# The SSM groups' matrix products in plain float32, with a shorter table of steps, in a hybrid encoder layer

## The chip, the cores and the metric

The kernel runs on one core of one Trainium2 chip. The time is device microseconds from the start to the end of an execution; the table below gives the median of three runs, and the profiled execution has a time of its own.

## The reference, cut to what matters

One encoder layer on an input of 4096 tokens and 1024 channels, all float32. A combined projection feeds three branches (a state space model, a pooling branch, windowed attention); their gated outputs are joined and projected back. The change concerns the first branch alone: 16 groups of 16 channels, each with 64 complex states in two directions.

```python
h = rms_norm(x, pre_g)
su, sg, pu, pg, q, k, v, ag = jnp.split(h @ w_in, IN_SPLITS, axis=-1)
...
bu_re = jnp.einsum('blgp,gnp->blgn', u, bb_re)
bu_im = jnp.einsum('blgp,gnp->blgn', u, bb_im)
_, _, h_re, h_im = lax.associative_scan(
    _complex_linear_combine, (lam_re, lam_im, bu_re, bu_im), reverse=reverse, axis=1)
return (jnp.einsum('blgn,gpn->blgp', h_re, c_re)
        - jnp.einsum('blgn,gpn->blgp', h_im, c_im))
...
y = jnp.concatenate([y_ssm, y_pool, y_attn], axis=-1) @ w_out
return x + rms_norm(y, post_g)
```

## The kernel before, in words

The tokens are cut into 8 blocks of 512. Matrix products keep close to float32 accuracy by splitting each operand into a high part of type float32r and the rest, a low part, and adding three products: high by high, high by low, low by high. `split` (line 187) does that: a copy on ACT writes the high part, and `lo_part` (line 184) subtracts it on DVE or, where the call says so, on POOL. `mm3` (line 989, its products on lines 990 to 992) issues the three products.

The program runs in four phases: two of input projections (the second with the attention), the remaining gate projections (`p3_block`, line 1129), and the output products (`w_out_k`, line 1278, lines 1287 to 1289) with the final norm. An order written by hand interleaves them: `Slots` (from line 84) holds a queue of steps for each slot, and `e.step()` issues the steps of one slot. `chunk` (line 354) issues six projection products of 128x512 and then takes one step, so a slot is six products of PE and whatever was queued for it. Each engine executes its instructions in the order in which they were issued.

`to_p3` (line 1397) runs at slot 422 and queues the 16 groups by `ssm_group` (line 994), each starting `SSM_PACE`, 8, slots after the one before it. The table at the end of `ssm_group` says which step of a group is issued how many slots after its start. Eight consecutive tokens form a chunk, so that a group works on tiles of 128 partitions by `NC`, 512, columns: `load` brings a record `rec` (the group's matrices and angles) and the input `u` by two DMAs on SP's queue; `inputs_hi`, `wb_lo`, `ur_lo` split both; `turns` (POOL) and the `angle_` steps (ACT) make cosines and sines `cs`; `inputs_mm` makes the real and imaginary inputs `vr` and `vi` in PSUM, `direct_mm` starts the output `y`; `turn_re`, `turn_im`, `turn_sum` rotate them (four products on DVE, two sums on POOL); `scan` runs the recurrence along the columns, two instructions of 64 partitions each time (lines 1069 and 1071, DVE); `back_cos` (DVE), `back_sin` and `back_sum` (POOL) rotate back; `state_hi`, `state_lo` split the states `h`; `state_mm` adds their products to `y`; `out_copy` and `store` bring it out. In the trace `tt` shows as line 162 and `copy` as line 173.

The gate projections run from slot 384 to 575, the output products from slot 576. Near the end of that phase `y_pool` (line 1172, started at slot 546) and `y_attn` (line 1209) put the pooling branch's and the attention's operands together on POOL, DVE and ACT, and `load_wo` (line 1115) loads and splits the weights of the output product. Of other parts the text names `pr` (line 451) and `kp` (lines 659 and 661), two places where the program before already multiplies plain float32 operands, of 128 columns.

Of the kernel before, what the change touches and what calls it, by code (L numbers as in the profile page):

```python
# [11 lines left out]
F32R = mybir.dt.float32r  # L12
# [4 lines left out]
P = 128  # L17
# [8 lines left out]
NC = SEQ // L  # L26
# [9 lines left out]
REC = 689  # L36
# [93 lines left out]
def hybrid_kernel(ctx, tc, A, out):  # L130
    nc = tc.nc
    V, S, PL, T = nc.vector, nc.scalar, nc.gpsimd, nc.tensor
    dma = nc.sync.dma_start
# [4 lines left out]
    swd = tc.dram_tile([G, P, REC], F32, name="swd")  # L138
# [22 lines left out]
    def tt(eng, out, in0, in1, op):  # L161
        return eng.tensor_tensor(out=out, in0=in0, in1=in1, op=op)  # L162
# [9 lines left out]
    def copy(out, in_):  # L172
        return S.activation(out=out, in_=in_, func=AF.Copy)  # L173

    def bank(i, shape, nm):
        return banks[i].tile(shape, F32, tag="b", name=nm)

    def bc(ap, shape):
        return ap.to_broadcast(shape)

    def f(ap):
        return ap.bitcast(F32)

    def lo_part(lo, src, hi, eng):
        tt(eng, lo, src, f(hi), ALU.subtract)

    def split(hi, lo, src, eng, lag=1, scale=None):

        copy(hi, src)
        if lag:  # L190
            e.at(e.now + lag, lo_part, lo, src, hi, eng)
        else:
            lo_part(lo, src, hi, eng)
# [795 lines left out]
    def mm3(o, wh, wl, r, first, last):  # L989
        T.matmul(o, lhsT=wh, rhs=r[:, 0], start=first, stop=False)  # L990
        T.matmul(o, lhsT=wh, rhs=r[:, 1], start=False, stop=False)
        T.matmul(o, lhsT=wl, rhs=r[:, 0], start=False, stop=last)

    def ssm_group(g, R, t0):


        sv = R["sv"]
        rho = bc(R["rho"][:, g:g + 1], [P, NC])
        X = {}

        def new(nm, shape, dt=F32, bufs=1):
            X[nm] = sv.tile(shape, dt, tag=nm, name=nm, bufs=bufs)
            return X[nm]

        def load():
            dma(out=new("rec", [P, REC], bufs=2), in_=swd[g])
            dma(out=new("u", [P, NC], bufs=2), in_=udram[g].rearrange("q s c -> s q c"))

        def inputs_hi():
            copy(new("ur", [P, 2, NC], F32R, 2)[:, 0], X["u"])  # L1010
            copy(new("wb", [P, 2, 3, P], F32R, 2)[:, 0], X["rec"][:, 0:384].rearrange("p (m c) -> p m c", m=3))

        def wb_lo():
            w = X["wb"]
            lo_part(w[:, 1], X["rec"][:, 0:384].rearrange("p (m c) -> p m c", m=3), w[:, 0], V)

        def turns():
            shc = [P, 16, 32]  # L1020
            rec = X["rec"]
            tt(PL, new("ang", shc), bc(rec[:, 672:688].unsqueeze(2), shc), bc(rec[:, 640:672].unsqueeze(1), shc),
               ALU.add)

        def ur_lo():
            lo_part(X["ur"][:, 1], X["u"], X["ur"][:, 0], PL)

        def angle_abs():
            cs = new("cs", [P, 2, NC], bufs=2)
            av = X["ang"].rearrange("p a b -> p (a b)")  # L1030
            S.activation(out=cs[:, 0], in_=av, func=AF.Abs)
            S.activation(out=cs[:, 1], in_=av, func=AF.Abs, bias=cst[:, C_NQ:C_NQ + 1])

        def angle_fold():
            S.activation(out=X["cs"], in_=X["cs"], func=AF.Abs, bias=cst[:, C_NHALF:C_NHALF + 1])

        def angle_sin():
            S.activation(out=X["cs"], in_=X["cs"], func=AF.Sin, scale=-TURN, bias=cst[:, C_HPI:C_HPI + 1])

        def inputs_mm():  # L1040
            w, ur = X["wb"], X["ur"]
            for i, nm in enumerate(("vr", "vi")):
                X[nm] = bank(4 + i, [P, NC], nm)
                mm3(X[nm], w[:, 0, i], w[:, 1, i], ur, True, True)

        def direct_mm():
            w = X["wb"]
            X["o"] = bank((6, 7, 2, 3)[g % 4], [P, NC], "y")
            mm3(X["o"], w[:, 0, 2], w[:, 1, 2], X["ur"], True, False)

        def turn_re():
            wt, t2 = new("wt", [P, 2, NC], bufs=2), new("t2", [P, 2, NC])
            tt(V, wt[:, 0], X["vr"], X["cs"][:, 0], ALU.mult)
            tt(V, t2[:, 0], X["vi"], X["cs"][:, 1], ALU.mult)

        def turn_im():
            wt, t2 = X["wt"], X["t2"]
            tt(PL, wt[:, 0], wt[:, 0], t2[:, 0], ALU.add)
            tt(V, wt[:, 1], X["vi"], X["cs"][:, 0], ALU.mult)
            tt(V, t2[:, 1], X["vr"], X["cs"][:, 1], ALU.mult)  # L1060

        def turn_sum():
            tt(PL, X["wt"][:, 1], X["wt"][:, 1], X["t2"][:, 1], ALU.subtract)
            wc = new("wc", [P, 2, 2, P], F32R, 2)
            split(wc[:, 0], wc[:, 1], X["rec"][:, 384:640].rearrange("p (m c) -> p m c", m=2), V)

        def scan(i):
            gs, wt = R["gs"][g % 2], X["wt"]
            V.tensor_tensor_scan(out=gs[0:64, i, 1:NC], data0=rho[0:64, 0:NC - 1], data1=wt[0:64, i, 0:NC - 1],  # L1069
                                 initial=0.0, op0=ALU.mult, op1=ALU.add)  # L1070
            V.tensor_tensor_scan(out=gs[64:128, i, NC - 2::-1], data0=rho[64:128, 0:NC - 1],  # L1071
                                 data1=wt[64:128, i, NC - 1:0:-1], initial=0.0, op0=ALU.mult, op1=ALU.add)

        sh2 = [P, 2, NC]

        def back_cos():
            tt(V, X["wt"], R["gs"][g % 2], bc(X["cs"][:, 0].unsqueeze(1), sh2), ALU.mult)

        def back_sin():
            tt(PL, R["gs"][g % 2], R["gs"][g % 2], bc(X["cs"][:, 1].unsqueeze(1), sh2), ALU.mult)  # L1080

        def back_sum(i):
            tt(PL, X["wt"][:, i], X["wt"][:, i], R["gs"][g % 2][:, 1 - i], ALU.add if i else ALU.subtract)

        def state_hi(i):
            copy(new(f"h{i}", [P, 2, NC], F32R)[:, 0], X["wt"][:, i])

        def state_lo():
            for i in range(2):
                h = X[f"h{i}"]  # L1090
                lo_part(h[:, 1], X["wt"][:, i], h[:, 0], V)

        def state_mm(i):
            wc = X["wc"]
            mm3(X["o"], wc[:, 0, i], wc[:, 1, i], X[f"h{i}"], False, i == 1)

        def out_copy():
            copy(new("yg", [P, NC], bufs=2), X["o"])

        def store():  # L1100
            dma(out=ybuf[g].rearrange("q s c -> s q c"), in_=X["yg"])

        for t, fn, a in ((0, load, ()), (3, inputs_hi, ()), (4, wb_lo, ()), (6, turns, ()), (7, ur_lo, ()),
                         (8, angle_abs, ()), (9, angle_fold, ()), (10, angle_sin, ()), (11, inputs_mm, ()),
                         (12, direct_mm, ()), (12, turn_re, ()), (13, turn_im, ()), (14, turn_sum, ()),
                         (15, scan, (0,)), (16, scan, (1,)), (18, back_cos, ()), (19, back_sin, ()),
                         (22, back_sum, (0,)), (23, back_sum, (1,)), (25, state_hi, (0,)), (26, state_hi, (1,)),
                         (27, state_lo, ()), (29, state_mm, (0,)), (30, state_mm, (1,)), (31, out_copy, ()),
                         (33, store, ())):
            e.at(t0 + t, fn, *a, label="ssm")  # L1110

    WO = {}
# [284 lines left out]
    def to_p3():  # L1397
        e.settle("p2")
        R2["ph"].close()
        R3.update(p3_open())  # L1400
        for g in range(G):
            ssm_group(g, R3, e.now + int(SSM_PACE * g))
# [115 lines left out]
```

## Time and profile before

| what | value |
|---|---|
| median of 3 runs | 1667.59 us (1665.9 to 1668.29) |
| the profiled execution | 1664.75 us |
| its span, first to last instruction | 1663.0 us |
| PE matmul records | 7364 |
| DVE, ACT, POOL instructions | 2047, 1624, 382 |

PE is the engine of matrix products, PEld its weight loads, DVE, ACT and POOL the three elementwise engines, SP the queue that issues most DMAs. A record of PE lasts from its issue to its modelled end and overlaps the next one, so the cost of a product in a stream is the distance between two starts. `fp32r` in a row is the type float32r; PE's rows write f32 for both kinds.

### The profile page before, as it was taken

The numbers are of one execution on the slowest core, as the hardware profiler recorded it, in microseconds if no ns is written. First come the engines' busy times: TensorE is split into PE (matmuls) and PEld (weight loads), VectorE is DVE, ScalarE is ACT, GpSimd is POOL, SyncE is SP. The second block draws the span as 40 slices with busy tenths as digits, with TensorE's granted clock in tenths as the row PEclk, the third lists the DMA queues.
The fourth block names the chain that finished last, engine by engine and source line by source line (L and its number), as shares of the span: only waits on it lengthen the run. The fifth ranks groups of instructions, "written<-read, shape, count | busy, mean of one in ns | idle before, by whom it ended". The sixth has DMA issues, their size and how long they took to land.

```text
span 1663.0 us, 20965 instructions
## 1 busy us (share of the span) xinstructions
PE 1574.8 (95%) x7364; PEld 1296.1 (78%) x7364; DVE 1152.4 (69%) x2047; ACT 766.5 (46%) x1624; POOL 665.0 (40%) x382
## 2 busy tenths in 40 slices
PE   8999899999999999999999989888879999999998
PEld 6787678888888888888888777676667788888886
DVE  5764676437777777777877399999985665555451
ACT  5424333346666666666776343433433333323221
POOL 0322122203233333233332277777752555555542
PEclk8999999999999999999999999999989999999999
DMA  6598999861111312123322655454635545555542
GB/s 227 174 301 262 285 302 309 290 237 63 64 64 64 118 66 71 64 75 116 133 89 89 209 182 169 121 176 144 207 122 183 188 156 176 176 179 179 176 152 76
DMA packets 131694, 267.60 MB, mean 161 GB/s; under 512 B 32386, under 2 KB 65922, under 8 KB 119812
## 3 DMA queue, kind: packets, MB, share of 16 engines
q1 hardware_dynamic: 126020, 251.57, 46.6%
q10 hardware_dynamic: 5568, 14.68, 2.6%
q8 instruction: 58, 0.95, 0.2%
q14 instruction: 48, 0.39, 0.1%
HBM read 173.25 MB, written 94.01 MB: 161 GB/s over the span
## 4 chain that ended last, share of the span: by engine, by line
PE 57%; DVE 22%; DMA 11%; issue 4%; POOL 4%; ACT 2%; SPq 1%; ACTq 0%; DVEq 0%; POOLq 0%
PE mm L350 7%; PE mm L351 7%; PE mm L352 7%; PE po L848 5%; DMA xs<-in_x_dram 5%; PE tp L858 5%; PE o L1289 5%; PE o L1287 5%; PE o L1288 5%; DVE gs L1069 4%; DVE gs L1071 4%; PE mm L361 4%; DVE h L162 3%; PE s L819 3%; PE s L818 3%
## 5 line engine op out<-in xcount | busy, mean ns | idle before, releaser
L350 PE MATMUL mm<-xk,w 128*128 128x512 f32 x968 | 388.3, 401 | 1.2 <-ACT xk L268 1.2
L351 PE MATMUL mm<-xk,w 128*128 128x512 f32 x968 | 383.5, 396 | 0.0
L352 PE MATMUL mm<-xk,w 128*128 128x512 f32 x968 | 382.1, 395 | 0.8 <-DVE w L162 0.8
L162 POOL TENSOR_TENSOR ns<-ns,es 128x1536 f32<-128x1536 f32 (+1 forms) x64 | 172.5, 2695 | 410.2 <-ACT pp L173 186.4
L352 PEld LDWEIGHTS mm<-xk,w 128*128 128x128 f32 x968 | 184.3, 190 | 41.9 <-DVE w L162 1.6
L350 PEld LDWEIGHTS mm<-xk,w 128*128 128x128 f32 x968 | 185.0, 191 | 36.6 <-ACT xk L268 1.9
L351 PEld LDWEIGHTS mm<-xk,w 128*128 128x128 f32 x968 | 184.7, 191 | 34.7 <-DVE xk L165 1.0
L820 DVE CUSTOM_DVE_ANT_0 ns<-s,cst,nsink 128x384 f32<-128x384 f32 (+1 forms) x256 | 145.7, 606 | 84.8 <-PE s L819 84.1
L1287 PE MATMUL o<-wo,yk 128*128 128x512 f32 x512 | 201.1, 393 | 3.0 <-ACT gg L1147 2.6
L1289 PE MATMUL o<-wo,yk 128*128 128x512 f32 x512 | 200.9, 392 | 2.1 <-DVE yk L165 2.1
L1288 PE MATMUL o<-wo,yk 128*128 128x512 f32 x512 | 200.4, 391 | 0.0
L173 ACT ACTIVATE pp<-tp 128x512 fp32r<-128x512 f32 x188 | 112.3, 597 | 170.6 <-PE tp L858 169.8
L361 PE MATMUL mm<-xk,w 128*128 128x512 f32 x552 | 149.3, 410 | 14.4 <-DVE xk L162 5.4
L809 ACT ACTIVATE ns<-ns,nm 128x384 f32<-128x384 f32 (+1 forms) x256 | 152.3, 598 | 2.0 <-DVE nm L820 2.0
L162 DVE TENSOR_TENSOR pp<-tp,pp 128x512 fp32r<-128x512 f32 x188 | 129.1, 687 | 18.8 <-ACT pp L173 17.4
L361 PEld LDWEIGHTS mm<-xk,w 128*128 128x128 f32 x552 | 103.3, 194 | 43.5 <-ACT xk L173 8.1
L848 PE MATMUL po<-pp,vr 128*128 128x512 f32 x376 | 127.8, 421 | 0.0
L162 POOL TENSOR_TENSOR xk<-xt,xk 128x512 fp32r<-128x512 f32 x32 | 51.8, 1625 | 172.8 <-ACT xk L173 111.0
L858 PEld LDWEIGHTS tp<-cst,ns 128*128 128x128 f32 x752 | 93.0, 140 | 34.6 <-issue 10.1
L858 PE MATMUL tp<-cst,ns 128*128 128x128 f32 x752 | 112.7, 272 | 7.3 <-DVE pp L162 7.3
L1287 PEld LDWEIGHTS o<-wo,yk 128*128 128x128 f32 x512 | 96.9, 189 | 24.4 <-ACT gg L1147 3.0
L1289 PEld LDWEIGHTS o<-wo,yk 128*128 128x128 f32 x512 | 96.9, 189 | 23.1 <-DVE yk L165 2.6
(293 smaller groups left out, 2795.3 us busy)
## 6 DMA issues: line engine op xcount, KB each, us to landing
xk<-xd SPq DMA_DIRECT2D x60, 1024.0 KB
xd<-xk SPq DMA_DIRECT2D x32, 1024.0 KB
xt<-in_xT_dram SPq DMA_DIRECT2D x35, 512.0 KB
xres<-in_x_dram SPq DMA_DIRECT2D x32, 512.0 KB
out_dram<-ot SPq DMA_DIRECT2D x31, 512.0 KB
xs<-in_x_dram ACTq DMA_DIRECT2D x24, 512.0 KB
raw<-in_w_in_dram SPq DMA_DIRECT2D x32, 256.0 KB
yattn<-ysb SPq DMA_DIRECT2D x32, 256.0 KB
```

The lines of the kernel that those rows point to most:

```text
L162: return eng.tensor_tensor(out=out, in0=in0, in1=in1, op=op)
L350: T.matmul(o, lhsT=w[:, 0, k], rhs=xh, start=(k == 0), stop=False)
L351: T.matmul(o, lhsT=w[:, 0, k], rhs=xl, start=False, stop=False)
L352: T.matmul(o, lhsT=w[:, 1, k], rhs=xh, start=False, stop=(k == NK - 1))
L361: T.matmul(o, lhsT=w[:, i, k], rhs=XK[b, k][h], start=(n == 0), stop=(n == 3 * NK - 1))
L809: S.activation(out=ns[:, hh, :nk], in_=ns[:, hh, :nk], func=AF.Exp, scale=-1.0, bias=nm[:, hh:hh + 1], accum_out=su[:, hh:hh + 1])
L820: V.tensor_tensor_reduce(out=ns[:, hh, :nk], in0=sp_[:, :nk], in1=cst[:, C_D + c0:C_D + c0 + nk], scale=-(2.0 ** -(h + 1)), scalar=R["nsin ...
L848: T.matmul(po, lhsT=VR[:, (ta + kb) % 8, kv], rhs=pp[:, i], start=(kb == 0 and i == 0), stop=(kb == nkb - 1 and i == 1))
L858: T.transpose(tp[:, hh], ns[:, hh, kb * P:(kb + 1) * P], ident)
L1287: T.matmul(o, lhsT=y[:, 0, ts_], rhs=WO[kk][:, 0, hs], start=first, stop=False)
L1288: T.matmul(o, lhsT=y[:, 0, ts_], rhs=WO[kk][:, 1, hs], start=False, stop=False)
L1289: T.matmul(o, lhsT=y[:, 1, ts_], rhs=WO[kk][:, 0, hs], start=False, stop=last)
```

## The change

In `ssm_group` all products take their operands as they lie in memory: `rec` and `u` for the inputs and the direct part, `rec` and `wt` for the states. One float32 `matmul` stands where `mm3` stood. The splits go: three copies' worth of high parts before the inputs (`ur`, `wb`), the split of `wc`, and the states' `h`. `rec` is held until the state products and has four buffers instead of two. The steps behind the removed ones move up: the inputs' products from step 11 to 9, the state products from 29 and 30 to 24 and 25, the store from 33 to 28.

```diff
--- before.py
+++ after.py
@@ -1003,16 +1003,8 @@
             return X[nm]
 
         def load():
-            dma(out=new("rec", [P, REC], bufs=2), in_=swd[g])
+            dma(out=new("rec", [P, REC], bufs=4), in_=swd[g])
             dma(out=new("u", [P, NC], bufs=2), in_=udram[g].rearrange("q s c -> s q c"))
-
-        def inputs_hi():
-            copy(new("ur", [P, 2, NC], F32R, 2)[:, 0], X["u"])
-            copy(new("wb", [P, 2, 3, P], F32R, 2)[:, 0], X["rec"][:, 0:384].rearrange("p (m c) -> p m c", m=3))
-
-        def wb_lo():
-            w = X["wb"]
-            lo_part(w[:, 1], X["rec"][:, 0:384].rearrange("p (m c) -> p m c", m=3), w[:, 0], V)
 
 
 
@@ -1022,9 +1014,6 @@
             tt(PL, new("ang", shc), bc(rec[:, 672:688].unsqueeze(2), shc), bc(rec[:, 640:672].unsqueeze(1), shc),
                ALU.add)
 
-        def ur_lo():
-            lo_part(X["ur"][:, 1], X["u"], X["ur"][:, 0], PL)
-
         def angle_abs():
             cs = new("cs", [P, 2, NC], bufs=2)
             av = X["ang"].rearrange("p a b -> p (a b)")
@@ -1038,15 +1027,13 @@
             S.activation(out=X["cs"], in_=X["cs"], func=AF.Sin, scale=-TURN, bias=cst[:, C_HPI:C_HPI + 1])
 
         def inputs_mm():
-            w, ur = X["wb"], X["ur"]
             for i, nm in enumerate(("vr", "vi")):
                 X[nm] = bank(4 + i, [P, NC], nm)
-                mm3(X[nm], w[:, 0, i], w[:, 1, i], ur, True, True)
+                T.matmul(X[nm], lhsT=X["rec"][:, 128 * i:128 * i + 128], rhs=X["u"], start=True, stop=True)
 
         def direct_mm():
-            w = X["wb"]
             X["o"] = bank((6, 7, 2, 3)[g % 4], [P, NC], "y")
-            mm3(X["o"], w[:, 0, 2], w[:, 1, 2], X["ur"], True, False)
+            T.matmul(X["o"], lhsT=X["rec"][:, 256:384], rhs=X["u"], start=True, stop=False)
 
         def turn_re():
             wt, t2 = new("wt", [P, 2, NC], bufs=2), new("t2", [P, 2, NC])
@@ -1061,8 +1048,6 @@
 
         def turn_sum():
             tt(PL, X["wt"][:, 1], X["wt"][:, 1], X["t2"][:, 1], ALU.subtract)
-            wc = new("wc", [P, 2, 2, P], F32R, 2)
-            split(wc[:, 0], wc[:, 1], X["rec"][:, 384:640].rearrange("p (m c) -> p m c", m=2), V)
 
         def scan(i):
             gs, wt = R["gs"][g % 2], X["wt"]
@@ -1082,17 +1067,9 @@
         def back_sum(i):
             tt(PL, X["wt"][:, i], X["wt"][:, i], R["gs"][g % 2][:, 1 - i], ALU.add if i else ALU.subtract)
 
-        def state_hi(i):
-            copy(new(f"h{i}", [P, 2, NC], F32R)[:, 0], X["wt"][:, i])
-
-        def state_lo():
-            for i in range(2):
-                h = X[f"h{i}"]
-                lo_part(h[:, 1], X["wt"][:, i], h[:, 0], V)
-
         def state_mm(i):
-            wc = X["wc"]
-            mm3(X["o"], wc[:, 0, i], wc[:, 1, i], X[f"h{i}"], False, i == 1)
+            T.matmul(X["o"], lhsT=X["rec"][:, 384 + 128 * i:512 + 128 * i], rhs=X["wt"][:, i], start=False,
+                     stop=(i == 1))
 
         def out_copy():
             copy(new("yg", [P, NC], bufs=2), X["o"])
@@ -1100,13 +1077,11 @@
         def store():
             dma(out=ybuf[g].rearrange("q s c -> s q c"), in_=X["yg"])
 
-        for t, fn, a in ((0, load, ()), (3, inputs_hi, ()), (4, wb_lo, ()), (6, turns, ()), (7, ur_lo, ()),
-                         (8, angle_abs, ()), (9, angle_fold, ()), (10, angle_sin, ()), (11, inputs_mm, ()),
-                         (12, direct_mm, ()), (12, turn_re, ()), (13, turn_im, ()), (14, turn_sum, ()),
-                         (15, scan, (0,)), (16, scan, (1,)), (18, back_cos, ()), (19, back_sin, ()),
-                         (22, back_sum, (0,)), (23, back_sum, (1,)), (25, state_hi, (0,)), (26, state_hi, (1,)),
-                         (27, state_lo, ()), (29, state_mm, (0,)), (30, state_mm, (1,)), (31, out_copy, ()),
-                         (33, store, ())):
+        for t, fn, a in ((0, load, ()), (3, turns, ()), (5, angle_abs, ()), (6, angle_fold, ()),
+                         (7, angle_sin, ()), (9, inputs_mm, ()), (10, direct_mm, ()), (10, turn_re, ()),
+                         (11, turn_im, ()), (12, turn_sum, ()), (13, scan, (0,)), (14, scan, (1,)),
+                         (16, back_cos, ()), (17, back_sin, ()), (20, back_sum, (0,)), (21, back_sum, (1,)),
+                         (24, state_mm, (0,)), (25, state_mm, (1,)), (26, out_copy, ()), (28, store, ())):
             e.at(t0 + t, fn, *a, label="ssm")
 
     WO = {}
```

DVE, one group in the steady part of the stage (`wb`, `wc`, `h` are split operands, `t` a temporary, `gs` the scan's result). Before:

```order
L162 TENSOR_TENSOR wt<-vr,cs 128x512
L162 TENSOR_TENSOR t_9394<-vi,cs 128x512
L162 TENSOR_TENSOR wb<-rec,wb 128x384
L162 TENSOR_TENSOR wt<-vi,cs 128x512
L162 TENSOR_TENSOR t_9394<-vr,cs 128x512
L1069 SCALAR_TENSOR_TENSOR gs_8795<-rho,wt 64x511
L1071 SCALAR_TENSOR_TENSOR gs_8795<-rho,wt 64x511
L162 TENSOR_TENSOR wc<-rec,wc 128x256
L1069 SCALAR_TENSOR_TENSOR gs_8795<-rho,wt 64x511
L1071 SCALAR_TENSOR_TENSOR gs_8795<-rho,wt 64x511
L162 TENSOR_TENSOR wt<-gs_8795,cs 128x1024
L162 TENSOR_TENSOR h_9468<-wt,h_9468 128x512
```

After the change:

```order
L162 TENSOR_TENSOR wt<-vr,cs 128x512
L162 TENSOR_TENSOR t_9282<-vi,cs 128x512
L162 TENSOR_TENSOR wt<-vi,cs 128x512
L162 TENSOR_TENSOR t_9282<-vr,cs 128x512
L1054 SCALAR_TENSOR_TENSOR gs_8795<-rho,wt 64x511
L1056 SCALAR_TENSOR_TENSOR gs_8795<-rho,wt 64x511
L1054 SCALAR_TENSOR_TENSOR gs_8795<-rho,wt 64x511
L1056 SCALAR_TENSOR_TENSOR gs_8795<-rho,wt 64x511
L162 TENSOR_TENSOR wt<-gs_8795,cs 128x1024
```

The subtractions of `wb`, `wc` and `h` are gone; a group's turns, scans and cosine product now stand together.

POOL, one group in the same part (`gs` by the sines, the two turn sums with `t`, `ang` of a later group, the two sums with `gs`). Before:

```order
L162 TENSOR_TENSOR gs_8795<-gs_8795,cs 128x1024
L162 TENSOR_TENSOR wt<-wt,t_9275 128x512
L162 TENSOR_TENSOR wt<-wt,gs_8795 128x512
L162 TENSOR_TENSOR wt<-wt,t_9275 128x512
L162 TENSOR_TENSOR ang<-rec 128x512
L162 TENSOR_TENSOR wt<-wt,gs_8795 128x512
L162 TENSOR_TENSOR ur<-u,ur 128x512
```

After the change:

```order
L162 TENSOR_TENSOR gs_8795<-gs_8795,cs 128x1024
L162 TENSOR_TENSOR wt<-wt,t_9380 128x512
L162 TENSOR_TENSOR ang<-rec 128x512
L162 TENSOR_TENSOR wt<-wt,gs_8795 128x512
L162 TENSOR_TENSOR wt<-wt,t_9380 128x512
L162 TENSOR_TENSOR wt<-wt,gs_8795 128x512
```

The subtraction of `ur` is gone, and `ang` stands ahead of the first sum with `gs`.

PE, around the inputs' products of the second group (`mm` is a gate projection; line 361 is the first chunk of a block). Before:

```order
L352 MATMUL mm<-xk,w 128x512
L990 MATMUL vr<-ur,wb 128x512
L991 MATMUL vr<-ur,wb 128x512
L992 MATMUL vr<-ur,wb 128x512
L990 MATMUL vi<-ur,wb 128x512
L991 MATMUL vi<-ur,wb 128x512
L992 MATMUL vi<-ur,wb 128x512
L350 MATMUL mm<-xk,w 128x512
L351 MATMUL mm<-xk,w 128x512
```

After the change, around those of a later group, with the last state product of an earlier group ahead of them:

```order
L351 MATMUL mm<-xk,w 128x512
L352 MATMUL mm<-xk,w 128x512
L1071 MATMUL y<-wt,rec 128x512
L1032 MATMUL vr<-u,rec 128x512
L1032 MATMUL vi<-u,rec 128x512
L361 MATMUL mm<-xk,w 128x512 x6
L1036 MATMUL y<-u,rec 128x512
```

Six products for `vr` and `vi` became two, and the state product directly ahead is the one of the group whose `wt` is to be written next.

## Rows read from the trace of the kernel before

**Rows 1.** The page's engine table: busy us, share of the span, instructions.
```profile
PE 1574.8 (95%) x7364; PEld 1296.1 (78%) x7364; DVE 1152.4 (69%) x2047; ACT 766.5 (46%) x1624; POOL 665.0 (40%) x382
```

**Rows 2.** Busy time by stretch: PE, PEld, DVE, ACT, POOL, then PEclk, DMA share, GB/s.
```profile
1000.00:1020.00 20.00, 16.98 (x62) 13.39 (x61) 19.76 (x15) 7.28 (x12) 15.47 (x9) 0.83 0.39 123
```

**Rows 3.** Timeline of DVE over one group: start, duration (us), engine, line, operation.
```profile
1003.01 1.09 DVE L162 TENSOR_TENSOR wc<-rec,wc 128x256 fp32r<-128x256 f32 x1
1004.03 2.30 DVE L1069 TENSOR_TENSOR_SCAN gs<-rho,wt 64x511 f32<-64x511 f32 x1
...
1008.52 1.23 DVE L162 TENSOR_TENSOR wt<-gs,cs 128x1024 f32<-128x1024 f32 x1
1009.66 3.47 DVE L162 TENSOR_TENSOR h<-wt,h 128x512 fp32r<-128x512 f32 x2
...
1014.47 0.55 DVE L162 TENSOR_TENSOR wb<-rec,wb 128x384 fp32r<-128x384 f32 x1
1014.93 0.68 DVE L162 TENSOR_TENSOR wt<-vi,cs 128x512 f32<-128x512 f32 x1
...
1020.71 1.10 DVE L162 TENSOR_TENSOR wc<-rec,wc 128x256 fp32r<-128x256 f32 x1
```

**Rows 4.** Waits in 960:1220, then 1195:1345: us in total, times, longest.
```profile
PE vr L991 <- POOL ur L162: 30.2, 14, 3.6
...
PE y L991 <- DVE h L162: 9.6, 1, 9.6
```

**Rows 5.** Timelines of PE and ACT: first, last group; next phase. Brackets: idle before.
```profile
938.78 3.06 PE L361 MATMUL mm<-xk,w 128*128 128x512 f32 x12 [2.01 <-ACT gg L1147]
941.67 0.39 PE L990 MATMUL vr<-ur,wb 128*128 128x512 f32 x1
...
937.20 0.63 ACT L173 ACTIVATE ur<-u 128x512 fp32r<-128x512 f32 x1 [10.68 <-DMA u<-udram]
...
1201.54 0.40 PE L990 MATMUL vr<-ur,wb 128*128 128x512 f32 x1
...
1251.38 0.39 PE L1287 MATMUL o<-wo,yk 128*128 128x512 f32 x1
```

**Rows 6.** Timeline of PE: first of each triple of `o`, 22 triples apart.
```profile
1260.63 0.39 PE L1287 MATMUL o<-wo,yk 128*128 128x512 f32 x1
...
1275.59 0.39 PE L1287 MATMUL o<-wo,yk 128*128 128x512 f32 x1
```

**Rows 7.** Float32 products of 128 columns on PE (one row: ns min/median/max); busy time around.
```profile
43.31 1.05 PE L451 MATMUL pr<-cst,rstd 128*128 128x128 f32 x8
...
L451 PE MATMUL pr<-cst,rstd x16: 271/275/363, 43.3 to 57.8; 128*128 128x128 f32 x16
...
140.27 0.64 PE L659 MATMUL kp<-obr,bz 128*64 128x128 f32 x2
140.69 0.63 PE L661 MATMUL kp<-obi,bz 128*64 128x128 f32 x2
...
43.00:45.00 2.00, 2.00 (x15) 1.79 (x14) 1.22 (x2) 0.60 (x2) 0.00 (x0) 1.00 0.12 47
139.20:142.00 2.80, 2.66 (x14) 2.47 (x14) 2.80 (x6) 2.28 (x5) 2.65 (x1) 0.60 0.86 355
```

**Rows 8.** Timelines of DVE and POOL: single, then one group on POOL.
```profile
949.20 1.20 DVE L1069 TENSOR_TENSOR_SCAN gs<-rho,wt 64x511 f32<-64x511 f32 x1
...
944.01 1.29 POOL L162 TENSOR_TENSOR wt<-wt,t 128x512 f32<-128x512 f32 x1 [4.83 <-DVE t L162]
...
1001.86 1.96 POOL L162 TENSOR_TENSOR ang<-rec 128x512 f32<-128x512 f32 x1
...
1009.82 2.76 POOL L162 TENSOR_TENSOR gs<-gs,cs 128x1024 f32<-128x1024 f32 x1 [2.42 <-DVE wt L162]
1014.69 1.48 POOL L162 TENSOR_TENSOR wt<-wt,t 128x512 f32<-128x512 f32 x1 [2.11 <-DVE t L162]
...
1017.38 2.21 POOL L162 TENSOR_TENSOR wt<-wt,t 128x512 f32<-128x512 f32 x1
```

## The prediction, made before the result was known

> **What bounds the kernel now.** The engine table of the page comes first [rows 1]: PE is busy for 95% of the span, so the first guess is that only PE's work counts. Busy time by stretches of 20 us corrects this for the stage that the change edits, the groups of the SSM (about 940 to 1250 us): in 1000:1020 DVE is busy for 19.76 us of 20 and PE for 16.98, at a granted clock of 0.83 [rows 2]. DVE sets the pace there, and PE waits. The timeline of DVE over one group shows the period: from one `wc` subtraction at 1003.01 to the next at 1020.71 are 17.70 us [rows 3]. The waits say who pays: PE stood 30.2 us, 14 times, before the second product of a group until POOL's `ur` subtraction was done, and 9.6 us once, near the end, for `h` [rows 4]. From the first group's first product (941.67) to the last group's (1201.54) are 259.9 us, 17.32 a group; the first product of the next phase starts at 1251.38 [rows 5].
>
> **The change part by part.**
>
> *Work taken off DVE.* Two `h` subtractions, 3.47 us together; `wc` from 1003.01 to the next start at 1004.03, 1.02; `wb` from 1014.47 to 1014.93, 0.46 [rows 3]. That is 4.95 us a group, all on the path, and leaves DVE 17.70 - 4.95 = 12.75. They are this dear because they meet POOL: POOL's `gs` product ran beside the `h` subtractions, and a scan that takes 2.30 us beside POOL took 1.20 when POOL had nothing to do [rows 3, 8].
>
> *Work taken off POOL and ACT.* POOL loses `ur`, and with it PE's 30.2 us go. ACT loses five copies a group; it is busy for 7.28 us of 20 [rows 2], so the five copies cost nothing now and bring nothing. What covers ACT's remaining work is PE's stream.
>
> *Work on PE.* Fifteen products of 128x512 become five in float32. A product of the old kind costs what `o` shows: 22 triples from 1260.63 to 1275.59 are 0.680 us a triple, 0.2267 each [rows 6]. The float32 price at 512 columns has no row; rows with 128 columns bound it. `pr` is issued as plain float32 products and leaves two records for each: 8 records last 1.05 us, a single one 0.27, so seven starts lie in 0.78, 0.111 a record, 0.22 a product, at clock 1.00 [rows 7]. Four times the columns: 0.89. `kp` repeats every 0.42 us, 140.27 to 140.69, in a stretch whose mean clock is 0.60 [rows 7]; read as the half clock (1.2 of 2.4 GHz), that is 1.68 for 512 columns, and 0.84 at full clock. If `pr` were held up by weight loads and not by its columns, a record could cost as little as an old product: 2 x 0.2267 = 0.45. I take 0.87, between the two full-clock readings, and keep 0.45 and 1.68 as ends.
>
> *The new period.* Eight slots hold 48 other products: 48 x 0.2267 = 10.88 us; with 5 x 0.87 = 4.35 PE needs 15.23, above DVE's 12.75. PE becomes the bound. Next behind it is the ring in which DVE and POOL work by turns: POOL's `gs` 2.76 and first sum 1.48, then `ang` 1.96, a sum 1.48 and a sum 2.21 beside the first pair of scans, then the second pair 2 x 2.30 and the cosine product 1.14 (1008.52 to 1009.66) make 15.6 by contended rows [rows 3, 8]. With `ur`, `wc` and `h` gone it must be shorter, so I take 15.23.
>
> *The shorter table.* A group's first product moves from step 11 to step 9, two slots: 12 x 0.2267 = 2.72 us. PE's wait of 2.01 us just before it, for ACT, which itself had waited for `u`, goes too. 941.67 - 4.73 = 936.94, but `u` landed only at 937.2 [rows 5], so 937.3. On SP's queue the two loads stay at step 0 and the store goes from 33 to 28. A load's first reader is now nine steps, some 17 us, behind it; the longest wait that ACT had for `u`, at the very start, was 10.68 [rows 5], so landing stays covered. Were it not, each group would pay the rest. Step 25 now reads `rec`, which is why it has four buffers.
>
> *The tail.* From the last group's first product to the next phase lie 22 slots and nine triples: 132 x 0.2267 + 9 x 0.68 = 36.0 us, but it took 49.8. Of the 13.8 of waiting 9.6 are the one for `h` [rows 4, 5]: the pooling steps' work on POOL and DVE stands in front of the last two groups. After: 24 slots and seven products, 144 x 0.2267 + 7 x 0.87 = 38.7. The pooling steps stay where they are, and the chain behind them loses `h`; I keep half the waiting, 6.9, with ends 0 and 13.8.
>
> *Sum.* 937.3 + 15 x 15.23 + 38.7 + 6.9 = 1211.4 instead of 1251.4: 40.0 us. The 411 us behind it, output products, are not edited and taken as they were. The profiled execution took 1664.75, so 1624.75; the median of the runs shown is 2.84 higher: **1627.6 us**. The tail's ends move it by 6.9 either way, a product of 0.84 or 0.89 us by 82 x 0.03 = 2.5 down or 1.6 up: its own range is 1618 to 1637.
>
> **Rivals.**
>
> *The ring of DVE and POOL decides.* Without contention POOL has 1.0 + 4 x 1.29 + 2.0 = 8.2 us, 1.29 being a sum with DVE idle, 1.0 and 2.0 my estimates for `ang` and `gs`, half of 1.96 and twice that; DVE has 4 x 1.20 + 1.14 = 5.9 [rows 3, 8]. If the two never overlap, 14.1. If DVE's four products from PSUM (4 x 0.68) had to stay clear of POOL too, 16.8: 15 x 1.59 = 23.9 us more, **1651.5**. For it: the doubled scans. Against: `wt` took 0.68 at 1014.93 with POOL running [rows 3, 8]. The Trainium skill, "SBUF — State Buffer", section "SBUF: two separate sides", has DVE and GpSimd share one port pair under an exclusive lock, the loser blocked for the whole instruction. The scan rows agree; by that rule alone, for operands in SBUF, the ring stays at 14.1, under PE.
>
> *Cheaper products.* At 0.45 PE needs 13.1 and the ring's 14.1 bounds: 15 x 1.13 = 17.0 us less, 2.9 in the tail and its 6.9 of waiting: **1600.8**. For it: `pr` streams only 128 columns beside each load of 128. Against: `kp` loads half as many weight columns, and its 0.42 us at half clock is still `pr`'s 0.22 twice [rows 7].
>
> *PE is the bound already, so its added work shows.* 80 x (0.87 - 0.68) = 15.2 us more than the median of before, **1682.8**. For it: the 95%. Against: PE's 16.98 of 20, and its 30.2 us of waits [rows 2, 4]. The Trainium skill, "FP8 and Floating Point Precision", section "TensorE Precision Notes", speaks for it: it counts four passes for true FP32, so four where there were three. As an estimate from that page a product would be 4 x 0.2267 = 0.91 and my own sum about 1631.
>
> *Half clock in the products.* PE needs more than the old period once a product costs (17.32 - 10.88) / 5 = 1.29 us. At `kp`'s 1.68 a group takes 19.28: 15 x 4.05 + 7 x 0.81 = 66 us above the forecast, **1694**. For it: the clock of 0.83 while the stage waits [rows 2]. Against: `pr` ran between other products at clock 1.00 [rows 7].
>
> **How the numbers follow.** The forecast has 0.62, the ring 0.15, cheap products 0.13, PE as the bound already 0.04, half clock 0.04; 0.02 stays for a gain that later waits give back, no change. 0.2%, 3.3 us, is about what a measurement can tell from none. So faster 0.90, same 0.02, slower 0.08. The range, 1604 to 1652, takes in the forecast's own, the ring, and the cheap case but for its far end.
>
> **What would show it.** Right: in 960:1160 PE near 20 us of 20 at clock 1.00 and DVE near 17; first products 15.2 us apart; two records, 0.43 us between starts, for each float32 product; no wait for `ur` or `h`; the first output product near 1211. Wrong: first products over 16 us apart while PE waits for POOL's `wt` (the ring); records over 0.6 us apart (the clock); or the 40 us back as waits after 1211, because the weights of the output product are not loaded in time.

## The result and the profile after

The changed kernel takes 1625.72 us (median of 4 runs, 1623.02 to 1630.12), the kernel before in the same comparison 1666.74 us (4 runs, 1664.34 to 1668.29). The ratio is 0.9756, with a 95% interval of 0.9731 to 0.978: faster by 41.0 us. The forecast was 1627.6 us. Of the runs below, the profiled execution of e5 ran at a mean clock of 0.557 and took 2593.36 us: its profile is not read, its median is that of the other three executions, and e9 is the same kernel.

The profiled execution is the longest of the four, 1630.12 us with a span of 1628.3. Its engine table, which answers to [rows 1]:

```profile
PE 1570.8 (96%) x7284; PEld 1273.6 (78%) x7284; DVE 1064.6 (65%) x1983; ACT 731.1 (45%) x1544; POOL 620.4 (38%) x366
```

The share of PE hardly moved, 95% to 96%. As before the change, only the stretch of the groups tells more. Busy time there, in the columns of [rows 2]:

```profile
1000.00:1020.00 20.00, 20.00 (x75) 13.66 (x73) 14.10 (x14) 6.21 (x9) 13.65 (x8) 1.00 0.63 188
...
1080.00:1100.00 20.00, 20.00 (x79) 14.43 (x77) 14.97 (x13) 7.38 (x10) 14.92 (x10) 1.00 0.50 171
```

PE went from 16.98 of 20 us to 20.00, at clock 1.00 instead of 0.83, and DVE from 19.76 to 14 or 15. The bound has changed hands. PE's timeline dates it: the first group's first product, the float32 products of a later slot, the last group's first product, the second state product of the group before it, and the first output products.

```profile
940.46 1.10 PE L1032 MATMUL vr<-u,rec 128*128 128x512 f32 x2 [0.19 <-PE mm L352]
...
969.61 1.02 PE L1071 MATMUL y<-wt,rec 128*128 128x512 f32 x2
970.47 1.02 PE L1032 MATMUL vr<-u,rec 128*128 128x512 f32 x2
971.33 1.02 PE L1032 MATMUL vi<-u,rec 128*128 128x512 f32 x2
...
1168.92 1.02 PE L1032 MATMUL vr<-u,rec 128*128 128x512 f32 x2
...
1186.14 1.12 PE L1071 MATMUL y<-wt,rec 128*128 128x512 f32 x2 [2.64 <-POOL wt L162]
...
1211.26 0.39 PE L1262 MATMUL o<-wo,yk 128*128 128x512 f32 x1
...
1218.15 0.79 PE L1262 MATMUL o<-wo,yk 128*128 128x512 f32 x1 [6.05 <-ACT gg L1122]
```

Products in a row start 0.86 us apart, each with two records (`x2`). From 940.46 to 1168.92 are 228.46 us, 15.23 a group. Cut at the places of [rows 5], the two profiled spans compare so (us):

| part | before | after | difference |
|---|---|---|---|
| start to the first product of the first group | 941.67 | 940.46 | -1.2 |
| 15 groups, first product to first product | 259.87 | 228.46 | -31.4 |
| last group's first product to the first `o` | 49.84 | 42.34 | -7.5 |
| first `o` to the end | 411.62 | 417.04 | +5.4 |
| span | 1663.0 | 1628.3 | -34.7 |

The profiled executions differ by 34.7 us and the medians by 41.0; the one of after was its kernel's longest, the one of before was near its shortest. The last row of the four gives 5.4 us back. The waits of PE behind 1212 show nearly all of it, in the columns of [rows 4]:

```profile
PE o L1262 <- ACT gg L1122: 6.0, 1, 6.0
...
PE z L991 <- DVE yr L165: 1.5, 2, 1.2
...
PE z L990 <- DVE ms L162: 0.4, 1, 0.4
```

The wait for `gg` was 2.6 us before, the waits of `z` were 0.3 in all. ACT's timeline shows what is late:

```profile
1216.04 0.63 ACT L173 ACTIVATE wo<-rawo 128x512 fp32r<-128x512 f32 x1 [5.99 <-DMA rawo<-in_w_out_dram]
1216.58 1.04 ACT L173 ACTIVATE yk<-ya 128x1024 fp32r<-128x1024 f32 x1
1217.52 0.58 ACT L1122 ACTIVATE gg<-mm 128x512 f32<-128x512 f32 x1
```

`gg` empties the bank of PSUM that the next output product needs, and it stands in ACT's order behind a copy of output weights that waits 5.99 us for its DMA. In the trace of before the same copy waited 3.34 us.

DVE over one group, to be laid beside [rows 3], and POOL over the same stretch:

```profile
998.83 1.23 DVE L162 TENSOR_TENSOR wt<-gs,cs 128x1024 f32<-128x1024 f32 x1
1002.17 0.69 DVE L162 TENSOR_TENSOR wt<-vr,cs 128x512 f32<-128x512 f32 x1 [2.11 <-PE vr L1032]
...
1005.01 2.05 DVE L1054 TENSOR_TENSOR_SCAN gs<-rho,wt 64x511 f32<-64x511 f32 x1 [0.20 <-POOL wt L162]
1007.07 2.16 DVE L1056 TENSOR_TENSOR_SCAN gs<-rho,wt 64x511 f32<-64x511 f32 x1
1010.35 2.30 DVE L1054 TENSOR_TENSOR_SCAN gs<-rho,wt 64x511 f32<-64x511 f32 x1 [1.12 <-POOL wt L162]
1012.66 1.22 DVE L1056 TENSOR_TENSOR_SCAN gs<-rho,wt 64x511 f32<-64x511 f32 x1
1013.92 1.23 DVE L162 TENSOR_TENSOR wt<-gs,cs 128x1024 f32<-128x1024 f32 x1
```

```profile
1000.20 2.36 POOL L162 TENSOR_TENSOR gs<-gs,cs 128x1024 f32<-128x1024 f32 x1 [3.71 <-DVE wt L162]
1003.70 1.28 POOL L162 TENSOR_TENSOR wt<-wt,t 128x512 f32<-128x512 f32 x1 [1.14 <-DVE t L162]
...
1008.11 2.20 POOL L162 TENSOR_TENSOR wt<-wt,t 128x512 f32<-128x512 f32 x1
1010.28 1.29 POOL L162 TENSOR_TENSOR wt<-wt,gs 128x512 f32<-128x512 f32 x1
```

DVE now waits for PE (2.11 us for `vr`), and the fourth scan runs after POOL's last sum has ended (1011.57) and takes 1.22 us instead of some 2.2. POOL's first sum and `gs`, 1.48 and 2.76 before [rows 8], take 1.28 and 2.36. The waits of 930:1215 count DVE's:

```profile
POOL gs L162 <- DVE wt L162: 53.4, 15, 3.9
DVE wt L162 <- PE vr L1032: 31.0, 15, 2.3
...
PE y L1071 <- POOL wt L162: 2.6, 1, 2.6
```

PE's 30.2 us for `ur` and 9.6 for `h` [rows 4] are gone; what is left of that kind is one wait of 2.6 us for `wt` of the last group but one.

### The profile page after: what moved, and what is told of

It is laid out like the page before. It is cut to its first block, busy times and chain, and to the rows that moved or that the text cites. A ratio compares the mean times of both kernels' runs of the same rounds, so it can differ in the third digit from the quotient of the medians.

```text
span 1628.3 us, 20646 instructions
## 1 busy us (share of the span) xinstructions
PE 1570.8 (96%) x7284; PEld 1273.6 (78%) x7284; DVE 1064.6 (65%) x1983; ACT 731.1 (45%) x1544; POOL 620.4 (38%) x366
## 4 chain that ended last, share of the span: by engine, by line
PE 67%; DMA 15%; DVE 8%; issue 4%; POOL 3%; ACT 2%; SPq 1%; ACTq 0%; POOLq 0%; DVEq 0%
PE mm L350 9%; PE mm L351 9%; PE mm L352 9%; DMA xs<-in_x_dram 7%; PE po L848 5%; PE mm L361 5%; PE tp L858 5%; PE o L1264 5%; PE o L1262 5%; PE o L1263 5%; PE s L819 3%; PE s L818 3%; PE y L1071 1%; POOL ot L162 1%; DMA rawo<-in_w_out_dram 1%
```

## The experiments

The theory: DVE set the period of the kernel before, PE sets the period now, and the ring of DVE and POOL lies under it. The rivals: PE bounds before too, so that products always cost; the ring bounds now; the float32 products are cheaper or dearer than 0.87; the shorter table earns the gain. Medians, each with its ratio to the kernel before on the same chip, and the cuts of the profiled span (us):

| run | median | ratio, 95% interval | period | tail | behind it |
|---|---|---|---|---|---|
| e1, float32 input products twice | 1651.65 | 0.991 [0.9891, 0.993] | 16.86 | 44.32 | 414.64 |
| e2, kernel before, input products twice | 1666.05 | 0.9998 [0.9984, 1.0011] | 17.38 | 49.99 | 411.46 |
| e3, one float32r product each | 1611.15 | 0.9668 [0.9642, 0.9695] | 13.95 | 45.48 | 414.72 |
| e4, old table of steps | 1630.44 | 0.9783 [0.9756, 0.9811] | 15.09 | 45.50 | 414.57 |
| e5, input splits kept | 1619.71 | 0.973 [0.9714, 0.9747] | | | |
| e6, state splits kept | 1643.9 | 0.9878 [0.9862, 0.9895] | 15.87 | 52.79 | 412.27 |
| e7, gate evacuated first | 1623.28 | 0.9745 [0.973, 0.9759] | 15.18 | 41.72 | 413.51 |
| e8, e7 and pooling earlier | 1620.76 | 0.9734 [0.972, 0.9749] | 15.50 | 40.66 | 409.37 |
| e9, e5 again | 1622.34 | 0.9744 [0.9728, 0.976] | 14.86 | 41.56 | 415.44 |
| e10, e5 with e8 | 1622.66 | 0.9748 [0.9732, 0.9763] | 15.33 | 37.00 | 412.61 |
| e11, the changed kernel again | 1627.33 | 0.9769 [0.9754, 0.9783] | 15.18 | 43.42 | 415.30 |
| e12, e5 with e7 | 1625.14 | 0.9748 [0.9734, 0.9761] | 14.87 | 41.53 | 414.93 |

### Which engine sets the pace: e1 and e2

e1 issues each of a group's two input products of the changed kernel twice, into the same bank:

```diff
                 T.matmul(X[nm], lhsT=X["rec"][:, 128 * i:128 * i + 128], rhs=X["u"], start=True, stop=True)
+                T.matmul(X[nm], lhsT=X["rec"][:, 128 * i:128 * i + 128], rhs=X["u"], start=True, stop=True)
```

> The changed kernel, with the two input products of a group (vr and vi) computed twice into the same bank: 32 more float32 products, the result unchanged. Theory (PE now sets the pace of the stage, a float32 product of 512 columns costs 0.855 us between starts): all of 32 x 0.855 = 27.4 us shows, the first products stand 16.9 us apart instead of 15.23, time 1653 us. Rival (the ring of DVE and POOL, which the order of steps ties together, sets the pace and PE only happens to be full): what DVE waits for vr now, 31.0 us in 15 waits, is the room that the repeat first uses up, it hides in part or whole, time 1626 to 1640 us.

e2 does the same to the kernel before:

```diff
                 mm3(X[nm], w[:, 0, i], w[:, 1, i], ur, True, True)
+                mm3(X[nm], w[:, 0, i], w[:, 1, i], ur, True, True)
```

> The kernel before, with the six products for vr and vi issued twice: 96 more float32r products, 21.8 us at 0.2267 us each, the result unchanged. Theory (DVE set the pace of the stage before, PE waited): PE's own need grows from 10.88 + 15 x 0.2267 = 14.28 to 15.64 us a group, still under 17.3, so 0 to 5 us of the 21.8 show, time 1667 to 1672 us. Rival (PE was the bound already): all of it shows, 1688 us.

Added work is 16 x 2 x 0.86 = 27.5 us of PE in e1 and 16 x 6 x 0.2267 = 21.8 us in e2. e1 is 25.9 us over the changed kernel, by medians: nearly all of it shows, in the period (16.86). e2 is 1.1 us under its own kernel before (1667.12), inside the interval: none of it shows. Busy time of e1, then of e2, in the stretch of [rows 2]:

```profile
1000.00:1020.00 20.00, 20.00 (x76) 13.81 (x75) 14.51 (x12) 5.13 (x7) 10.24 (x6) 1.00 0.58 176
```

```profile
1000.00:1020.00 20.00, 18.32 (x80) 14.73 (x79) 19.77 (x17) 7.97 (x14) 15.46 (x9) 1.00 0.37 123
```

In e2 DVE is as full as before, 19.77, and PE has used up a part of its waits:

```profile
PE vr L991 <- POOL ur L162: 20.8, 13, 2.0
```

That is 9.4 us of 30.2 [rows 4]. Most of the rest of the 21.8 came from the clock. Over 960:1160 PE was busy for 174.05 us in the kernel before and 182.98 in e2, 8.9 more for 11 x 1.36 = 15.0 of added products; the ten stretches of 20 us were granted between 0.83 and 1.00 before, and 1.00 in all but the first (0.91) in e2. So DVE was the bound and PE is: the rival by which PE bounded already falls. (What counts as DVE's busy time holds waits for POOL too, as the rows of e3 show next.)

### The ring of DVE and POOL: e3

e3 multiplies the high parts alone, one float32r product for each float32 one. It leaves out the two low products and their subtractions; the copies that write the high parts lie on ACT.

```diff
-                T.matmul(X[nm], lhsT=X["rec"][:, 128 * i:128 * i + 128], rhs=X["u"], start=True, stop=True)
+                T.matmul(X[nm], lhsT=X["wb"][:, i], rhs=X["ur"], start=True, stop=True)
...
+        def state_hi(i):
+            copy(new(f"h{i}", [P, NC], F32R, 2), X["wt"][:, i])
+
         def state_mm(i):
-            T.matmul(X["o"], lhsT=X["rec"][:, 384 + 128 * i:512 + 128 * i], rhs=X["wt"][:, i], start=False,
+            T.matmul(X["o"], lhsT=X["wb"][:, 3 + i], rhs=X[f"h{i}"], start=False,
```

> The changed kernel with only the high parts multiplied, one float32r product in place of each float32 one; the low parts of all operands are left out of the result. Four copies a group come back on ACT, nothing on DVE or POOL. PE's need falls to 10.88 + 5 x 0.2267 = 12.0 us a group. Theory with the ring close behind PE at about 14.1 us: first products 14 us apart, DVE and POOL waiting for each other, PE waiting for POOL's wt or vr's bank, time about 1605 us. Rival (nothing close behind PE): 12.7 us a group, DVE's own work, time about 1580 us.

PE needs only 53 x 0.2267 = 12.0 us a group here, and the period is 13.95. Busy time of e3 in 1080:1100, and DVE from one cosine product to the next:

```profile
1080.00:1100.00 20.00, 16.98 (x73) 13.21 (x72) 16.21 (x13) 11.99 (x19) 12.95 (x8) 1.00 0.58 188
```

```profile
1043.19 1.22 DVE L162 TENSOR_TENSOR wt<-gs,cs 128x1024 f32<-128x1024 f32 x1
...
1048.25 2.05 DVE L1058 TENSOR_TENSOR_SCAN gs<-rho,wt 64x511 f32<-64x511 f32 x1 [1.44 <-POOL wt L162]
1050.31 2.16 DVE L1060 TENSOR_TENSOR_SCAN gs<-rho,wt 64x511 f32<-64x511 f32 x1
1053.60 2.26 DVE L1058 TENSOR_TENSOR_SCAN gs<-rho,wt 64x511 f32<-64x511 f32 x1 [1.13 <-POOL wt L162]
1055.87 1.22 DVE L1060 TENSOR_TENSOR_SCAN gs<-rho,wt 64x511 f32<-64x511 f32 x1
1057.13 1.23 DVE L162 TENSOR_TENSOR wt<-gs,cs 128x1024 f32<-128x1024 f32 x1
```

POOL in the same stretch:

```profile
1048.17 1.05 POOL L162 TENSOR_TENSOR ang<-rec 128x512 f32<-128x512 f32 x1
1049.18 2.21 POOL L162 TENSOR_TENSOR wt<-wt,gs 128x512 f32<-128x512 f32 x1
1051.35 2.21 POOL L162 TENSOR_TENSOR wt<-wt,t 128x512 f32<-128x512 f32 x1
1053.52 1.27 POOL L162 TENSOR_TENSOR wt<-wt,gs 128x512 f32<-128x512 f32 x1
```

No engine is full, and DVE stands still only for POOL's sums, 1.44 and 1.13 us of 13.94. PE's waits for the copies of the states on ACT (17.9 us in 960:1160) don't reach it: DVE waited for `vr` once there, 0.5 us.

The two work by turns even where both look busy. Start plus duration gives the ends: `ang` 1049.22, scan 1050.30, sum 1051.39, scan 1052.47, sum 1053.56, each 1.08 or 1.09 us after the other engine's. The third scan starts while POOL's last sum runs and ends 1.07 us behind it (1054.79); the fourth, without POOL, takes 1.22. So a duration of 2.0 to 2.3 us is a wait for the other engine's operation and some 1.1 us of work. The kernel before shows the same from POOL's side: a scan started first, at 949.20, and took 1.20 [rows 8]; POOL's sum started 0.16 us later and ended 1.10 us behind it:

```profile
949.36 2.14 POOL L162 TENSOR_TENSOR wt<-wt,t 128x512 f32<-128x512 f32 x1 [4.06 <-DVE t L162]
```

That is the ring, at 13.95 where the prediction worked out 14.1 without contention and 16.8 at worst. It lies 1.3 us under PE's 15.23, so the rival by which it decides falls.

### What the table is worth: e4

e4 has the changed kernel's products at the step numbers of the kernel before (inputs' products at 11, state products at 29 and 30, store at 33).

> The changed kernel with the steps at the places of the old table (first products at step 11, state products at 29 and 30, store at 33), only the products changed. Theory (PE full from the first group to the end of the stage): the table only moves work along a stream that is full, period 15.23 us as now, the same total of products before the output products, time within 5 us of 1625.7. Rival (the latency from a group's first product to its output counts): five slots of 1.9 us, about 9.5 us more, 1635 us.

It took 1630.44 us, and its interval overlaps that of the changed kernel. In the profile the period is no longer (15.09), though DVE now waits for the old buffers of `wt`, which the later state products release late. Waits of e4 in 960:1160:

```profile
DVE wt L162 <- PE y L1071: 38.3, 12, 8.4
```

This is idle time of an engine that does not bound. What the table brings lies in the tail, 45.50 instead of 42.34 us; a few microseconds at most, not settled by these runs. Nearly all of the gain comes with the products.

### Which of the splits mattered: e5, e6 and e9

e6 takes the inputs in float32 and splits the states' operands as the kernel before did (`wc` and `h` on DVE, three products):

```diff
+            wc = new("wc", [P, 2, 2, P], F32R, 2)
+            split(wc[:, 0], wc[:, 1], X["rec"][:, 384:640].rearrange("p (m c) -> p m c", m=2), V)
...
+                lo_part(h[:, 1], X["wt"][:, i], h[:, 0], V)
...
+            mm3(X["o"], wc[:, 0, i], wc[:, 1, i], X[f"h{i}"], False, i == 1)
```

> The other half: the products of u in plain float32, the states still split, with h and wc on ACT and DVE, the state products at steps 27 and 28. PE needs 10.88 + 3 x 0.855 + 6 x 0.2267 = 14.8 us a group. Theory (DVE set the pace before, and h and wc are 4.5 of the 4.95 us that were taken off it): DVE near 17 us a group again less what POOL no longer takes from it, first products 15.8 to 17 us apart, time 1638 to 1658 us, most of the gain lost. Rival (ur on POOL, for which PE waited 30 us before, held the stage): 15 us apart, 1622 to 1628 us.

e5 and e9 are the counterpart: `ur` split with POOL and `wb` with DVE, three products for the inputs and the direct part at the old steps, and float32 for the states, at steps 26 and 27.

```diff
+            lo_part(w[:, 1], X["rec"][:, 0:384].rearrange("p (m c) -> p m c", m=3), w[:, 0], V)
...
+            lo_part(X["ur"][:, 1], X["u"], X["ur"][:, 0], PL)
...
-                T.matmul(X[nm], lhsT=X["rec"][:, 128 * i:128 * i + 128], rhs=X["u"], start=True, stop=True)
+                mm3(X[nm], w[:, 0, i], w[:, 1, i], ur, True, True)
```

> Half of the change: the state products in plain float32, the products of u still split, with ur on ACT and POOL and wb on ACT and DVE at their old steps, the state products at steps 26 and 27. PE needs 10.88 + 9 x 0.2267 + 2 x 0.855 = 14.6 us a group, a little less than the changed kernel. Theory (a ring of DVE and POOL of about 14 us is close behind PE, and ur's subtraction of 1.3 to 2.2 us on POOL and wb's 0.5 on DVE lengthen it): first products 15.3 to 16.5 us apart, PE waiting for ur, time 1628 to 1645 us. Rival (PE alone decides): 14.6 us apart, 1617 us.

> The same kernel as in e5 (inputs split, states in plain float32), run for a trace, since the profiled execution of e5 ran at half the clock throughout. Theory after e5 (PE alone decides even with ur back on POOL): first products 14.6 to 14.9 us apart, PE full, POOL near 16 of 20 us busy. Rival (the ring binds and the gain comes from the tail): 15.2 us or more apart, and a tail shorter by 5 us than the changed kernel's 42.3.

e6 loses 18.2 us of the 41.0. Its busy time, its waits of PE in 930:1300, and the returned `h`:

```profile
1000.00:1020.00 20.00, 19.34 (x78) 14.06 (x76) 19.52 (x15) 6.46 (x10) 13.59 (x7) 1.00 0.57 167
```

```profile
PE y L991 <- DVE h L162: 20.8, 23, 7.6
```

```profile
1049.88 3.48 DVE L162 TENSOR_TENSOR h<-wt,h 128x512 fp32r<-128x512 f32 x2
```

DVE is the bound again (19.52 of 20). The period of 15.87 is a mean of two parts: over its last ten groups the first products are 16.45 to 16.59 us apart, where the changed kernel has 15.25 to 15.27, and over the first five 13.50 to 15.27. And the longest wait for `h`, 7.6 us, is back in the tail (52.79).

e9 loses nothing: 1622.34 us beside 1627.33 for the changed kernel in e11, on the same chip, with intervals that touch. Its busy time, its wait for `ur`, and DVE's groups in 960:1160:

```profile
1000.00:1020.00 20.00, 20.00 (x85) 15.69 (x85) 19.93 (x17) 7.55 (x13) 17.80 (x10) 1.00 0.64 201
```

```profile
PE vr L991 <- POOL ur L162: 1.0, 2, 0.8
```

```profile
L162 DVE TENSOR_TENSOR wt<-gs,cs 128x1024 f32<-128x1024 f32 x13 | 27.6, 2122 | 0.4
L162 DVE TENSOR_TENSOR wb<-rec,wb 128x384 fp32r<-128x384 f32 x13 | 20.1, 1543 | 5.4 <-ACT wb L173 5.4
```

PE needs 57 x 0.2267 + 2 x 0.86 = 14.6 us a group and takes 14.86, with DVE as full as PE. So once `h` and `wc` are off DVE the input splits fit in at no cost: `ur` is still subtracted on POOL and PE waits 1.0 us for it, not 30.2. The 30.2 us had been the lateness of the whole stage, which PE met at `ur`. That does not make the input splits worthless by themselves: e6, which takes only them away (with the shorter table), is 21.5 us faster than its kernel before (1665.4), e9 42.7 faster than its own (1665.06). The halves do not add up, and no run separates `wb` on DVE from `ur` on POOL. The expectation by the theory for e5 missed: the subtractions fill DVE and POOL, but they don't lengthen the ring past PE's need. That DVE is so full here is contention: with POOL at 17.80 of 20, `wb` takes 1.54 us, which took 0.55 in [rows 3], and the cosine product 2.12 instead of 1.23.

### The 5 us that come back: e7, e8, e10 and e12

e7 puts the evacuation of the last gate projections a slot earlier, ahead of the copy that waits for its DMA:

```diff
-            e.at(e.now + 1, go)
+            e.at(e.now if s == NB - 1 else e.now + 1, go)
```

> The changed kernel with the gates of the last block brought out of PSUM one slot earlier, so that on ACT the last of them stands ahead of the copies that wait for the loads of the output product's weights and for POOL's attention product. Theory (the 6.0 us that PE waits for gg just after the first output product are that order on ACT): the wait shrinks below 2 us, 3 to 6 us less, time 1620 to 1623 us. Rival (the weights themselves are late): the wait moves to the next output product, which waits for the weights or the operands, time 1626 us.

e8 does that and starts the pooling steps 8 slots earlier:

```diff
-    e.at(b0 - 6, lambda: e.gen(e.now, y_pool(0, R3["psc"])), label="main")
+    e.at(b0 - 14, lambda: e.gen(e.now, y_pool(0, R3["psc"])), label="main")
```

> As the one before, and the first block's pooling steps start eight slots earlier, at slot 538. Theory (they stand on DVE and POOL ahead of the last two groups, cost PE 2.6 us of waiting for wt, and hold up the splits of the output weights behind them, so that the loads wait for buffers): another 2 to 5 us less, 1616 to 1620 us. Rival (they only move the same 8 us on POOL to earlier groups, where the ring has 1 us to spare): no gain, or up to 3 us more.

In e7 the wait for `gg` is gone, and part of it has moved on. Its waits of PE in 1205:1300:

```profile
PE z L990 <- ACT yr L1220: 2.6, 1, 2.6
...
PE z L991 <- DVE yr L165: 1.9, 1, 1.9
```

From the first `o` to the end it takes 413.51 us, not 417.04 or, in e11, 415.30: 1.8 to 3.5 of the 5.4 us. This shows what made the wait; but the median, 1623.28, does not stand apart from the changed kernel's. e8 brings the last part to 409.37 us and the tail to 40.66, and gives some back in one place. From the second interval on its first products are 15.25 to 15.27 us apart, as in the changed kernel, but the last interval is 19.77, which makes the mean 15.50:

```profile
1169.61 2.08 PE L1071 MATMUL y<-wt,rec 128*128 128x512 f32 x2 [3.34 <-DMA agate<-gg]
1171.47 1.91 PE L1032 MATMUL vr<-u,rec 128*128 128x512 f32 x2
1173.18 1.91 PE L1032 MATMUL vi<-u,rec 128*128 128x512 f32 x2
```

The row names a DMA, but `wt`'s sum, which stood on POOL behind 5.92 us of pooling sums, ended at 1169.55. Behind the wait the granted clock was 0.53 in 1168:1172 and 0.61 in 1172:1176 (the lower of its two levels, 1.2 and 2.4 GHz, for most of both), and the float32 products stand 1.71 us apart. The median of e8, 1620.76 us, is the lowest of the versions that split nothing. Its interval, 0.972 to 0.9749, overlaps the changed kernel's first one (0.9731 to 0.978) and lies just under that of e11 (0.9754 to 0.9783), which ran on another chip.

e10 and e12 join the two improvements, e5's split inputs with e8's and with e7's edits. e11 is the unedited changed kernel on the chip of e9 and e10.

> e5's split of inputs together with e8's order at the end of the stage (last gates one slot earlier, first pooling steps eight slots earlier). If the two gains are independent: 1620.7 - 5 = 1615.7 us. Rival (e8's pooling steps meet a ring that ur has made longer): 1619 to 1624 us.

> The changed kernel itself once more, beside the two above on one chip, to compare with them directly: 1623 to 1629 us by all explanations.

> e9's split of inputs (first products 14.86 us apart) with e7's earlier gates alone, the pooling steps left at slot 546. Theory (the two gains lie in different stretches, e9's in the groups and e7's 3 to 4 us just after the first output product): 1621.5 - 2.5 = 1619 us, the wait for gg under 2 us. Rival (what e7 takes from the wait for gg comes back as a wait for the next operands): 1622 us.

The gains, a few microseconds each, do not add: 1622.66 and 1625.14 us, where the sums were to give 1615.7 and 1619. In e10 the last interval is 22.53 us instead of 14.75, with waits of 3.0 and 1.6 us for `wt`, which lifts the period from 14.86 to 15.33. In e12 the cuts behind the first product are those of e9: the wait for `gg` (5.7 us in e9) is gone, and waits of 2.7 and 1.9 us for the operands of `z` stand in its place. Its groups began at 945.27 us, 5.8 later than in e9, in phases that neither edit touches. So no version is clearly shown to beat the changed kernel. The widest apart of those meant to are e5 (0.973) and e11 (0.9769), 0.39%, and e9, which is e5 again, has 0.9744.

## Why the prediction was right

- **The sum.** Forecast 40.0 us less, measured 41.0 by the medians, but 37.7 in the comparison of e11 and 34.7 between the two profiled executions. There the terms come out so: the first product 3.2 us too early, the period right, the tail 3.3 too long, the part behind it 5.4 too short (40.0 - 3.2 + 3.3 - 5.4 = 34.7). The mechanism and the period were right; that the median lies 1.9 us from the forecast is partly luck.
- **DVE was the bound, PE the next.** Shown by e2 (21.8 us of products hidden) and e1 (25.9 of 27.5 us seen). The engine table had said the opposite; busy time in the stage's own stretch and the waits said it right.
- **The float32 product.** Forecast 0.87 us, measured 0.86, in two records. `pr`, 128 columns wide, scaled by its columns as assumed. The low end, 0.45, was wrong, and the estimate of 0.91 was 0.05 too high. The half clock's 1.68 did not come, for the clock stayed at 1.00 in the groups; but e8's 1.71 shows that `kp` was read rightly.
- **The period.** Forecast 15.23 and measured 15.23 us; over 15 groups 228.5 and 228.46. The closeness flatters the sum a little: e11 had 15.18, and both have 15.25 to 15.27 from the second interval on and a shorter first one (14.76 and 14.01).
- **DVE's new need.** Forecast 12.75, from contended rows. Measured 11.4 (four scans, the cosine product and four products of 0.69 by their mean in 960:1160), since POOL no longer runs beside the fourth scan. "DVE near 17" was too high by the same amount, and it cost nothing because DVE is off the path.
- **The ring.** 14.1 was worked out, 13.95 measured in e3. The row of 1.20 [rows 8] was the right one to take, though the reading "when POOL had nothing to do" was not: POOL's sum began 0.16 us after that scan and waited for it. The Trainium skill, "SBUF — State Buffer", section "SBUF: two separate sides", by which DVE or GpSimd holds a shared port pair for a whole instruction and the other is blocked, agrees with the ends in e3 that follow each other by 1.07 to 1.09 us, and with the scan's 1.22 us without POOL and 2.30 beside it.
- **The wait for `ur`.** It went, but it would have gone with `ur` still on POOL: e9 keeps it there and waits 1.0 us. The prediction took `ur` itself for the cause, without harm to the sum, which stood on the period alone. Of DVE's 4.95 us, all put down as time on the path, `wb` costs nothing once `h` and `wc` are gone (e9); with these kept, 18.2 of the 41.0 us are lost (e6).
- **The first product.** Forecast 937.3, profiled 940.46. From the last product of the attention phase (`po`) to the first of the groups the time fell from 20.3 to 15.6 us, 4.7 where 4.4 were forecast; that phase ended 3.5 us later in this execution. e1, e6, e7 and e8 have 938.0 to 938.9, and e11, the changed kernel again, 939.26. "Nine steps" from a load to its first reader holds for `u` only: `rec` is first read by `turns`, at step 3. No wait of PE shows it.
- **The tail.** Forecast 45.6 us, measured 42.34: of the 6.9 us of waiting that I kept, 3.6 are left, the largest the 2.64 for `wt`.
- **Behind it.** "Taken as they were" was the term that failed: 417.04 us instead of 411.62 (415.30 in e11). The loads of the output weights are tied to PE's slots but not made faster by them, so the groups that end earlier meet them later; the prediction had named this sign, waits after 1211 for these weights, at no cost. Of the 5.4 us 3.4 are the longer wait for `gg` and 1.6 the longer waits of `z`. The tail's 3.3 us too much and these 5.4 too little nearly cancelled.

## What to carry to other kernels

When an elementwise engine bounds a stage that matrix products share, one plain float32 product (0.86 us here) in place of three split ones (0.68) can pay, because what counts is the subtraction that it spares the full engine: find which split that is, for once it is gone the others may stay at no cost. To learn which engine bounds, double some of its work and look whether the time follows. When two engines take turns, read the ends of their operations and not the durations, which hold the waiting. After a stage has been made faster, look at its end: an evacuation queued behind a copy that waits for a load hands back what was gained.

## What the runs showed of the hardware

- A plain float32 product of 128x128 by 512 columns leaves two records and takes 0.86 us of the stream at clock 1.00, 3.8 times a float32r product's 0.2267. At a granted clock of 0.53 to 0.61, behind a wait of 3.34 us in e8, two stood 1.71 us apart.
- The granted clock went with PE's waits: over 960:1160 it was below 1.00 in six of ten stretches before, where PE stood up to 3.6 us at a time, and 1.00 in all of them after. In e3 PE stood up to 1.5 us at a time there and kept 1.00. Of the products added in e2, about 6.1 of 15.0 us in 960:1160 were paid by the higher clock and not by idle time (15.0 less the 8.9 of added busy time), so PE had more room than its waits told.
- DVE's time for one operation follows what POOL does: the cosine product took 1.23 us in the changed kernel and 2.12 in the mean of e9, the scans 1.22 and 2.0 to 2.3. In e3 the two engines' operations end in turn, 1.07 to 1.09 us apart, and the waiting counts as busy time. The products that read PSUM took 0.68 us with POOL's `gs` running.
